# Preparing the next head's value and gate weights a head ahead, in a two-layer hybrid decoder step

## The chip, the cores and the metric

The kernel runs on one core of one Trainium2 chip. The metric is the device time of one execution in microseconds (us). The kernel before was run three times: median 2831.7 us, 2829.96 to 2833.98.

## What is computed

One step of a two-layer decoder over a prompt of 2048 positions and a sample group of 8 sequences with 4 positions each, at model width 1024, all in float32. Layer 0 is gated linear attention with 4 heads (key width 128, value width 512); layer 1 is sliding-window attention, which is not touched here. Of layer 0, cut to what matters:

```python
u = rmsnorm(h, norm_g)
proj = u @ w_in                                   # q, k, v, gate, g_low
log_a = log_sigmoid(g_low @ w_gate2 + b_gate) / 16
# for each head, chunk by chunk:
out       = (qc * exp(b)) @ state + scores @ vc
new_state = exp(b_last) * state + (kc * exp(b_last - b)).T @ vc
# then
o = rmsnorm(o, out_norm_g)
h = h + (o * silu(gate)) @ w_out
```

So each head needs its own 1024 x 512 slice of `w_in` for the values (v) and another for the gate (g), besides slices for q and k.

## The kernel before, in words

**Numbers.** Every float32 operand of a matrix product is split into two float16 parts, a high and a low one, and a product is three TensorE (PE) passes: high by high, high by low, low by high. A weight has to be *converted* so before its use: a float32 piece of 128 x 512 is loaded into one of three raw buffers (tag `wraw`), ScalarE (ACT) writes the high part, scaled by the norm's gain, and VectorE (DVE) writes the low part (`split`, lines 191 and 192, called from `Unit.convert`). A `Unit` is two such pieces, its two halves, and becomes a tile of 512 KB in one of 12 weight slots (tag `W`). The v weights of a head are four units, its gate weights four, its q and k weights together two.

**Two ways to a weight slot.** `Unit.load` converts straight into the slot. `Unit.prepare` converts each half into one of two staging buffers (tag `pst`) and writes it to a DRAM tile (`pre`) by a DMA issued from GpSimd (POOL, line 242). A unit that has been prepared answers `steps()` with a single fetch: one DMA of 512 KB from `pre` to a slot, issued from SyncE (SP). `Unit.load` and the fetch both wait until PE is done with the slot's earlier tile.

**Order of work.** Layer 0 goes through 16 blocks, four blocks of 512 positions for each of four heads (`blocks`). A block has four chunks of 128 positions. For a chunk, PE makes the v and gate projections (24 matmuls each, `vg_steps`), then the state product, the output and the state update, the norm, and the spill of the gated output (`chunk_steps`). In between, the next block's q and k projections and its seven decay levels (`level_steps`) are done. In the first three blocks of a head the two projections of a chunk run together; in a head's last block all v projections come first, then all gate projections, with the next head's v weights converted after the former and its gate weights after the latter. `weave(main, fill)` deals the closures of one list among those of another, and `mix` merges two lists in the same way. After a head's last block the 8 sample sequences of that head are done (`SampleA.steps`), woven into the first block of the next head; their state halves (`seq`) are split into the same two `pst` buffers.

**The list of conversions for later.** `prep` is a list of closures for work that layer 1 needs: eight rope tables, 72 halves of layer 1's input weights, and 64 steps that form combinations of its output weights, 144 in all. `some(n)` takes the next n. In the blocks of heads 0 to 3 the kernel takes `some(PR[j])` in each of three chunks of block j, with `PR = (1, 4, 2, 0)`: 3, 12 and 6 steps in the first three blocks of heads 1 and 2, 3 and 12 in head 3 (whose third block loads the output projection's weights instead), and 6 in the third block of head 0; 63 in all. The remaining 81 are dealt over the output projection of layer 0, seven a chunk from its fifth chunk on.

**What sets the order on the chip.** The program is built under a planner (`TileContext(nc, schedule_with_timeline_sim=True)`) that orders the instructions of each engine by priority against a simulated timeline; the closures' order gives the priorities, and `behind(steps, n)` lowers those of its steps by n. Only layer 1 pins PE's order. A tile takes the next buffer of its tag, and waits for those who use the earlier tile in that buffer. Each engine, and SP's queue of DMAs, runs its own instructions strictly in order.

Of the kernel before, what the change touches and what calls it, by code (L numbers as in the profile page):

```python
# [23 lines left out]
NBL = 4  # L24
KT = D // P
AH, DK, DV = 4, 128, 512
# [27 lines left out]
NV = 5  # L54
KL = 5
QL = 9
PR = (1, 4, 2, 0)


class Ctx:  # L60
# [14 lines left out]
def _body(tc, nc, cp, sb, ps, dr, i, o):  # L75
# [6 lines left out]
    def T(tag, shape, dt, bufs=None):  # L82
        return sb.tile(shape, dt, tag=tag, name=nm(tag), **({} if bufs is None else {"bufs": bufs}))
# [42 lines left out]
    def gain(t, src, load):  # L126
        load(t, src.rearrange("(k p) -> p k", p=P))
        dve.tensor_scalar(t, t, SW, None, ALU.mult)
# [16 lines left out]
    def weave(main, fill):  # L145

        main, fill = list(main), list(fill)
        done = 0
        for n, f in enumerate(main):
            f()  # L150
            upto = len(fill) * (n + 1) // len(main)
            for g in fill[done:upto]:
                g()
            done = upto
        for g in fill[done:]:
            g()

    def run(steps):
        for f in steps:
            f()  # L160

    def mix(a, b):

        out = []
        weave([lambda f=f: out.append(f) for f in a], [lambda f=f: out.append(f) for f in b])
        return out
# [214 lines left out]
    def u_steps(j):  # L381
        def chunk(c):
            if j > 0:
                t = T("W", [P, D], F32, NW)
                xh = [t[:, :512], t[:, 512:]]
            else:
                xh = [T("v", [P, 512], F32, 4) if c > 1 else T(tag, [P, 512], F32, 2) for tag in ("st", "sth")]
            for half in range(2):
                nc.sync.dma_start(xh[half], i["x_prompt"][0, j * 512 + c * P : j * 512 + (c + 1) * P, half * 512 : half * 512 + 512])
            norm_T(xh, P, lambda hl: uT[j][:, :, hl, c * P : (c + 1) * P], j == 0)  # L390

        return behind([lambda c=c: chunk(c) for c in range(4)], 20 if j > 0 else 0)
# [18 lines left out]
    def head_weights(h):  # L411
        w = HeadW()
        w.qk = [
            Unit([(0, P, w_in[u * 512 : u * 512 + 512, h * P : (h + 1) * P]), (P, P, w_in[u * 512 : u * 512 + 512, 512 + h * P : 512 + (h + 1) * P])], 256, gs_a, range(u * 4, u * 4 + 4))
            for u in range(2)
        ]
        w.q = lambda kt, hl: w.qk[kt // 4](kt % 4, hl, slice(0, P))
        w.k = lambda kt, hl: w.qk[kt // 4](kt % 4, hl, slice(P, 2 * P))
        w.v = Cols(w_in, 1024 + h * DV, 512, gs_a, KT)
        w.g = Cols(w_in, 3072 + h * DV, 512, gs_a, KT)  # L420
        return w
# [446 lines left out]
    def some(n=2):  # L868
        out = prep[:n]
        del prep[:n]  # L870
        return out
# [17 lines left out]
    hw = {0: head_weights(0)}  # L889
    cur = Blk(0, 0, hw[0])  # L890
# [14 lines left out]
    f = T("pst", [P, 7, 64], F32, 2)  # L905
# [16 lines left out]
    prev_tail = []  # L922
    samp = None
    sparts = []

    for n, (h, j) in enumerate(blocks):
        nxt = None
        if n + 1 < len(blocks):
            h2, j2 = blocks[n + 1]
            nxt = Blk(h2, j2, hw[h2])  # L930
        side = []
        if n == 0:
            side = u_steps(2)
        elif n == 1:
            side = u_steps(3) + [us_step]
        lv = nxt.level_steps() if nxt else []
        last = j == NBL - 1
        late = j == 0 and h > 0
        if n > 0:
            weave(cur.vg_steps(0, (0,) if late else (0, 1)), prev_tail)  # L940
        if last:
            samp = SampleA(h, cur.w)
            for f in samp.proj_steps():
                f()
        if nxt:
            for f in nxt.qk_steps():
                f()
        if late:
            weave(cur.vg_steps(0, (1,)), [])
        if last:  # L950
            ch = [cur.chunk_steps(c) for c in range(3)]
            weave([f for c in range(1, 4) for f in cur.vg_steps(c, (0,))], ch[0] + lv[:3] + ch[1][:3] + lv[3:5] + ch[2][:3])
            run(hw[h + 1].v.steps() if h + 1 < AH else wo.steps()[4:])
            for c in range(1, 4):
                weave(cur.vg_steps(c, (1,)), (ch[c - 1][3:] if c > 1 else []) + lv[3 + c * 2 : 5 + c * 2])
            for f in ch[2][3:]:
                f()
            run(hw[h + 1].g.steps() if h + 1 < AH else wo1.steps()[8:])
        else:
            for c in range(3):  # L960
                if n == len(blocks) - 2:
                    if c == 0:
                        wo_aside()
                    more = (wo1.steps()[:8] + wo.steps()[:4])[c * 4 : c * 4 + 4]
                else:
                    more = side[c * 2 : c * 2 + 2] if n < 2 else some(PR[j])
                weave(cur.vg_steps(c + 1, (0, 1) if n else (1,)), mix(cur.chunk_steps(c) + lv[(0,3,6)[c]:(3,6,8)[c]], sparts[(0,3,7)[c]:(3,7,99)[c]]) + more)
                if j == NBL - 2 and h + 1 < AH and c == 0:
                    hw[h + 1] = head_weights(h + 1)
                    for u in hw[h + 1].qk:  # L970
                        for f in u.steps():
                            f()
            sparts = []
        if n == 0:
            gain(gs_o, i["a_out_norm"][0], later)
            gain(gs_kv, i["kv_norm"], later)
            gain(gs_b, i["b_norm"][0], later)

            def bf_const(name, shape):
                f = T("pst", shape, F32, 2)  # L980
                later(f, i["c_" + name])
                t = C(name, shape, BF16)
                dve.tensor_copy(t, f)
                return t

            madd = bf_const("madd", [P, 2, P])
            nsink = C("nsink", [P, NKV * GRP], F32)
            later(nsink, i["b_sinks"][0].partition_broadcast(P))
            dve.tensor_scalar(nsink, nsink, -1.0, None, ALU.mult)
            gq = C("gq", [P, 2, HD], F32)  # L990
            for x_, g in enumerate((i["b_q_norm"][0], i["k_norm"])):
                later(gq[:, x_, :], g.partition_broadcast(P))

            lvs = C("lvs", [96, 2, 16], U8)
            f_ = T("pst", [96, 2, 16], F32, 2)
            later(f_, i["c_lvs"])
            dve.tensor_copy(lvs, f_)
            id3 = C("id3", [96, SMP], F32)
            later(id3, i["c_id3"])
            bm = C("bm", [96, NS], F32)  # L1000
            later(bm, i["c_bm"])
            onef = T("spp", [P, P], F32, 1)
            pool.memset(onef, 1.0)
            smask = bf_const("smask", [P, 2, 160])
            rts = C("rts", [SMP, 4, HD], F32)
            for y_ in range(2):
                for z_ in range(2):
                    x_ = 2 * y_ + z_
                    later(rts[:, x_, :], i["c_rope_s"][z_])
                    if z_ == 0:  # L1010
                        dve.tensor_tensor(rts[:, x_, :], rts[:, x_, :], gq[:SMP, y_, :], ALU.mult)
                    else:
                        H2 = HD // 2
                        dve.tensor_tensor(rts[:, x_, :H2], rts[:, x_, :H2], gq[:SMP, y_, H2:], ALU.mult)
                        dve.tensor_tensor(rts[:, x_, H2:], rts[:, x_, H2:], gq[:SMP, y_, :H2], ALU.mult)
            sel = T("sq1", [GRP, P], F32, 1)
            later(sel, i["c_sel"])
            skT = C("skT", [GRP, NKV], F32)
            later(skT, i["b_sinks"][0].rearrange("(g r) -> r g", r=GRP))
            psk = PT("tr", [P, NKV], bufs=2)  # L1020
            nc.tensor.matmul(psk, sel, skT, start=True, stop=True)
            sinkr = C("sinkr", [P, NKV], F32)
            dve.tensor_scalar(sinkr, psk, 8.0, None, ALU.mult)
        prev_tail = cur.chunk_steps(3) + (nxt.decay_steps() if nxt else [])
        if j == NBL - 1:
            sparts = samp.steps()
            prev_tail += sparts[:4]
            del sparts[:4]
            if nxt is None:
                prev_tail += sparts  # L1030
        cur = nxt
# [636 lines left out]
    for t in range(-3, NKV * NCH):  # L1668
        fill = []
        n = t + 3  # L1670
        if n < NKV * NCH:
            g, c = divmod(n, NCH)
# [55 lines left out]
    for p_ in range(NCH // 2):  # L1728
        more = []
        if p_ + 1 < NCH // 2:  # L1730
            nxt = pairs[p_ + 1]
            ld, sm = [lambda x=x, nxt=nxt: nxt.load(x) for x in (2, 3, 0, 1)], nxt.sums()
            more = ld[:2] + sm[:2] + ld[2:3] + sm[2:6]
# [3 lines left out]
        if p_ in (3, 4):  # L1737
            n = p_ - 3
# [87 lines left out]
```

## Time and profile before

| | |
|---|---|
| median of three runs | 2831.7 us |
| the profiled execution | 2836.73 us |
| its span, first to last instruction | 2834.9 us |
| mean granted TensorE clock | 0.986 |
| PE busy | 2716.0 us (96% of the span) |
| DVE, ACT, POOL busy | 1699.3, 1392.5, 1145.7 us |
| the 16 blocks of layer 0 end at | 1143.8 us |
| q and k, v and gate conversions of layer 0 (`wraw` from `a_w_in`) | 96 loads |
| write-outs of prepared weights (`pre` from `pst`) | 72, 256 KB each |
| fetches of prepared weights (`W` from `pre`) | 36, 512 KB each |

How it is read: a row of a table by stage has the stage's limits and length in microseconds from the span's start, then the busy time of each engine with the number of its instructions in brackets, then PE's granted clock, the busy share of the 16 DMA engines, and GB/s. When the table is asked for one tile, it counts the instructions that write or read that tile alone; an engine without any is left out, and a DMA issued by POOL counts as POOL's. A row of the waits has the engine and line that waited, what released it, then microseconds in total, times, and the longest. A row of the timeline has start, duration, engine, line, operation, out<-in, shapes and, in square brackets, how long the engine had been idle and who released it. L191 is line 191 of the kernel, and as `split` is a helper, its lines stand for every split; the tiles tell them apart.

### The profile page before, as it was taken

Reading aid. Unit: us, or ns where it says so; the run is one execution under the profiler, and the core shown is the slowest. Engines: PE = TensorE matmul, PEld = TensorE weight load, DVE = VectorE, ACT = ScalarE, POOL = GpSimd, SP = SyncE. Lnnn points to the kernel's source line nnn. Section 1 sums busy time; section 2 is a strip of 40 time slices with the busy share of each in tenths; the row PEclk is TensorE's granted clock in tenths of the full one; section 3 lists DMA queues with packets and bytes.
Section 4 is the critical chain, followed back from the end, with each engine's and each line's share of the span. In section 5 each row is a group of like instructions: output and inputs, shape, how many; then the busy total and the mean of one; then the engine's idle time right before and its main releaser. Section 6 shows DMA issues by size and latency. Waiting matters only on the chain.

```text
span 2834.9 us, 51733 instructions
## 1 busy us (share of the span) xinstructions
PE 2716.0 (96%) x19258; PEld 1388.1 (49%) x19258; DVE 1699.3 (60%) x3470; ACT 1392.5 (49%) x3245; POOL 1145.7 (40%) x1600
## 2 busy tenths in 40 slices
PE   6899998999899999999899999999999999989999
PEld 4444544544454445444344555555555555544444
DVE  5665666566657655335422665677777777777653
ACT  6554655455546553433322555566666666651110
POOL 2352244224323421125503686566567567530000
PEclk9999999999999999999999999999999999999999
DMA  8351334134313533799987678978888899996431
GB/s 210 87 128 35 101 105 148 34 86 138 116 38 86 167 90 81 184 214 260 258 183 190 129 146 152 226 133 157 187 149 151 155 189 185 177 220 201 154 99 57
DMA packets 801029, 411.69 MB, mean 145 GB/s; under 512 B 644352, under 2 KB 717896, under 8 KB 800744
## 3 DMA queue, kind: packets, MB, share of 16 engines
q1 hardware_dynamic: 787816, 372.66, 57.5%
q0 software_dynamic: 10880, 35.66, 3.7%
q8 instruction: 150, 2.46, 0.4%
q14 instruction: 103, 0.84, 0.1%
q10 hardware_dynamic: 2080, 0.07, 0.0%
HBM read 161.97 MB, written 107.54 MB: 95 GB/s over the span
## 4 chain that ended last, share of the span: by engine, by line
PE 60%; DMA 9%; ACT 9%; DVE 8%; issue 6%; POOL 5%; SPq 1%; ACTq 0%; POOLq 0%; DVEq 0%
PE pj L101 35%; PE o L101 11%; PE tr L101 9%; PE kv L101 3%; ACT o L1261 2%; DVE v L192 2%; DMA pre<-pst 1%; PE lev L101 1%; ACT v L191 1%; DMA wraw<-in_a_w_in_dram 1%; DVE o L1256 1%; POOL ogT L189 1%; DMA pst<-v 1%; DMA uT<-ogT 1%; DVE lev L1256 1%
## 5 line engine op out<-in xcount | busy, mean ns | idle before, releaser
L101 PE MATMUL pj<-W,uT 128*128 128x512 f16 x5088 | 1198.8, 381 | 6.2 <-ACT sg L481 3.6
L101 PEld LDWEIGHTS <-uT 128*128 128x128 f16 x6976 | 650.5, 98 | 711.3 <-issue 36.7
L101 PE MATMUL tr<-W,uT 128*128 128x512 f16 x1536 | 365.6, 379 | 0.0
L180 POOL TENSOR_SCALAR rs_m<-ss 128x1 f32<-128x1 f32 (+3 forms) x186 | 40.0, 215 | 537.0 <-DVE ss L1158 186.2
L101 PEld LDWEIGHTS <-X 128*128 128x128 f16 x2744 | 185.1, 98 | 141.5 <-issue 15.8
L1261 ACT ACTIVATE o<-o,mx 128x256 f32<-128x256 f32 (+1 forms) x384 | 168.7, 439 | 165.9 <-DVE mx L1256 162.0
L101 PE MATMUL pj<-uT,W 128*128 128x512 f16 (+1 forms) x912 | 190.2, 358 | 26.1 <-DMA uT<-ogT 22.6
L1256 DVE CUSTOM_DVE_ANT_0 o<-o,madd,nsink 128x256 f32<-128x256 f32 (+1 forms) x384 | 183.8, 479 | 38.6 <-PE o L101 34.2
L192 DVE SCALAR_TENSOR_TENSOR v<-o,v 128x512 f16<-128x512 f32 (+1 forms) x192 | 129.0, 672 | 104.4 <-ACT v L191 102.2
L181 POOL TENSOR_TENSOR rs_r<-rs_m,mhalf 128x1 f32<-128x1 f32 (+3 forms) x182 | 185.0, 1016 | 13.4
L514 POOL TENSOR_TENSOR KQ<-KQ,bt 128x256 f32<-128x256 f32 x112 | 97.7, 873 | 229.1 <-DVE X L189 229.1
L101 PEld LDWEIGHTS <-W 128*128 128x128 f16 x2448 | 129.6, 99 | 114.2 <-issue 23.2
L101 PEld LDWEIGHTS <-v 128*128 128x128 f16 x976 | 95.3, 98 | 116.4 <-issue 4.4
L189 POOL TENSOR_TENSOR ogT<-og,ogT 128x512 f16<-128x512 f32 x68 | 82.2, 1208 | 123.8 <-ACT ogT L188 123.8
L101 PEld LDWEIGHTS <-sg 128*128 128x128 f16 x800 | 78.4, 99 | 106.3 <-DMA sg<-ogd 11.7
L188 ACT ACTIVATE X<-KQ 128x512 f16<-128x512 f32 x128 | 84.6, 661 | 74.2 <-PE lev L101 46.8
L101 PE MATMUL o<-gl,X 128*128 128x256 f16 (+1 forms) x768 | 113.9, 271 | 3.1 <-DMA X<-qe 1.7
L189 DVE TENSOR_TENSOR X<-KQ,X 128x512 f16<-128x512 f32 x128 | 98.5, 770 | 28.4 <-ACT X L188 27.4
L191 ACT ACTIVATE v<-o 128x512 f16<-128x512 f32 (+1 forms) x192 | 111.1, 579 | 3.6
L242 POOL DMA_DIRECT2D pre<-pst x72 | 50.4, 702 | 142.2 <-DVE pst L192 111.7
L1261 ACT ACTIVATE lev<-lev,mx 128x256 f32<-128x256 f32 (+1 forms) x128 | 56.5, 441 | 103.6 <-DVE mx L1256 101.5
L101 PE MATMUL pj<-W,v 128*128 128x512 f16 x448 | 104.4, 379 | 0.4 <-DMA v<-ogd 0.4
(437 smaller groups left out, 4848.0 us busy)
## 6 DMA issues: line engine op xcount, KB each, us to landing
pre<-pst POOLq DMA_DIRECT2D x72, 256.0 KB, 3.4
W<-pre SPq DMA_DIRECT2D x36, 512.0 KB
ogd<-ogT SPq DMA_DIRECT2D x68, 256.0 KB
wraw<-in_a_w_in_dram SPq DMA_DIRECT2D x64, 256.0 KB
wraw<-in_b_w_in_dram SPq DMA_DIRECT2D x64, 256.0 KB
oge<-og SPq DMA_DIRECT2D x64, 256.0 KB
wraw<-in_a_w_out_dram SPq DMA_DIRECT2D x32, 256.0 KB
X<-in_x_prompt_dram SPq DMA_DIRECT2D x32, 256.0 KB
```

The source lines that it names most:

```text
L101: return order(nc.tensor.matmul(*a, **k))
L180: pool.tensor_scalar(m[:n, :k], ss, a, b, ALU.mult, ALU.add)
L181: pool.tensor_tensor(r[:n, :k], m[:n, :k], mhalf[:n, :k], ALU.pow)
L188: act(hi, src, AF.Copy)
L189: eng.tensor_tensor(lo, src, hi, ALU.subtract)
L191: act(hi, src, AF.Copy, scale=sc)
L192: dve.scalar_tensor_tensor(lo, src, sc, hi, ALU.mult, ALU.subtract)
L242: nc.gpsimd.dma_start(self.pre[:, :, half * 512 : half * 512 + 512], t)
L514: pool.tensor_tensor(keys, keys, d[:, :, 1:2].to_broadcast([P, NB, m]), ALU.mult)
L1256: dve.tensor_tensor_reduce(pm[:, z], pm[:, z], madd.rearrange("p a b -> p (a b)")[:, (2 - nk) * P :], -0.125, nsink[:, g * GRP + h : g * G ...
L1261: act(pm[:, z], pm[:, z], AF.Exp, scale=-1.0, bias=nm_[:, h : h + 1], accum_out=bx["sum"][:, h : h + 1])
```

## The change

`PR` goes. A list `ahead` holds the conversions that the coming blocks are to take. When head h's run begins (in its first block, for head 0 in its second), the next head's weights object is made, the 16 halves of its v and gate weights are put up for preparing, and they are mixed with steps of `prep`: 2 for head 0, 11 for heads 1 and 2. Head 3 takes 18 steps of `prep` alone. A head's last block takes 10 more (heads 0 to 2). Each chunk of the first three blocks takes three of them (`early(3)`), the last block five and then up to two a chunk. `hw[h + 1].v.steps()` and `.g.steps()` in the last block are unchanged in text, but as their units have been prepared, each is now a fetch. The q and k weights are loaded directly as before, at the same place. 120 steps are taken in the blocks, 48 of them the halves of v and gate weights, and 72 of `prep` are left for the output projection.

```diff
-PR = (1, 4, 2, 0)
...
+    ahead = []
...
         lv = nxt.level_steps() if nxt else []
+        if j == min(h, 1) ^ 1 and h + 1 < AH:
+            hw[h + 1] = head_weights(h + 1)
+            ahead = mix(hw[h + 1].v.prepare() + hw[h + 1].g.prepare(), some(11 if h else 2))
+        elif j == 0 and h > 0:
+            ahead = some(18)
+        elif j == NBL - 1 and nxt:
+            ahead = some(10)
+
+        def early(n):
+            out = ahead[:n]
+            del ahead[:n]
+            return out
+
...
-            weave([f for c in range(1, 4) for f in cur.vg_steps(c, (0,))], ch[0] + lv[:3] + ch[1][:3] + lv[3:5] + ch[2][:3])
+            weave([f for c in range(1, 4) for f in cur.vg_steps(c, (0,))], mix(ch[0] + lv[:3] + ch[1][:3] + lv[3:5] + ch[2][:3], early(5)))
             run(hw[h + 1].v.steps() if h + 1 < AH else wo.steps()[4:])
             for c in range(1, 4):
-                weave(cur.vg_steps(c, (1,)), (ch[c - 1][3:] if c > 1 else []) + lv[3 + c * 2 : 5 + c * 2])
+                weave(cur.vg_steps(c, (1,)), mix((ch[c - 1][3:] if c > 1 else []) + lv[3 + c * 2 : 5 + c * 2], early(2)))
...
-                    more = side[c * 2 : c * 2 + 2] if n < 2 else some(PR[j])
+                    more = mix(early(3), side[c * 2 : c * 2 + 2])
...
                 if j == NBL - 2 and h + 1 < AH and c == 0:
-                    hw[h + 1] = head_weights(h + 1)
                     for u in hw[h + 1].qk:
```

## The prediction

> **What bounds the kernel now.** I read the page first, then the busy time of each engine stage by stage (the edges are the gate activations that end a block, so each stage is one block of 512 positions of one head), then the same table for two tiles alone, then the waits and the timeline of one block.
>
> ```profile
> span 2834.9 us, 51733 instructions
> PE 2716.0 (96%) x19258; PEld 1388.1 (49%) x19258; DVE 1699.3 (60%) x3470; ACT 1392.5 (49%) x3245; POOL 1145.7 (40%) x1600
> ```
>
> TensorE is busy for 2716.0 of 2834.9 us, so all that any reordering of conversions can win is among 118.9 us of idle PE. The question is where these lie. In the table by stage the third number is the stage's length and the next PE's busy time:
>
> ```profile
> 143.60:206.40 62.80, 57.50 (x313) 26.50 (x312) 36.36 (x69) 34.59 (x68) 33.35 (x45) 0.97 0.57 130
> 206.40:270.30 63.90, 63.90 (x387) 30.89 (x385) 36.74 (x61) 31.23 (x56) 19.23 (x31) 1.00 0.15 41
> 270.30:337.70 67.40, 67.40 (x547) 34.65 (x546) 39.86 (x67) 37.96 (x70) 16.52 (x28) 1.00 0.22 67
> 337.70:405.80 68.10, 67.46 (x483) 33.77 (x482) 46.09 (x94) 43.32 (x77) 25.53 (x40) 1.00 0.39 113
> 405.80:480.30 74.50, 66.24 (x358) 30.57 (x356) 50.92 (x81) 46.28 (x79) 36.33 (x48) 0.98 0.55 173
> 480.30:542.60 62.30, 62.30 (x370) 29.69 (x369) 28.46 (x45) 20.42 (x38) 16.08 (x27) 1.00 0.08 22
> 542.60:608.90 66.30, 66.13 (x528) 33.73 (x526) 39.12 (x63) 37.29 (x68) 16.45 (x27) 1.00 0.23 67
> 681.50:753.30 71.80, 64.52 (x357) 30.20 (x356) 48.95 (x77) 40.58 (x72) 35.41 (x47) 1.00 0.57 180
> 815.70:882.00 66.30, 66.13 (x527) 33.71 (x526) 39.07 (x63) 37.46 (x67) 15.89 (x27) 1.00 0.26 66
> 953.00:1027.00 74.00, 66.03 (x359) 30.73 (x358) 49.25 (x77) 48.35 (x77) 33.81 (x44) 0.98 0.51 160
> 1143.80:1440.00 296.20, 279.88 (x1555) 129.56 (x1554) 129.45 (x190) 99.95 (x190) 104.56 (x140) 0.97 0.92 227
> ```
>
> Heads 1, 2 and 3 lose 8.26, 7.28 and 7.97 us in their second block (405.8, 681.5 and 953.0), together 23.5 us. Their last blocks, in which the next head's v and gate weights are converted today, lose 0.17 us each (head 0's at 270.3: nothing). So the work that the change takes out costs PE nothing where it stands. What differs in the second blocks is seen in the raw weight tile (ACT's x is the number of conversion pieces) and in the DRAM tile of prepared weights (POOL's x is the number of write-outs):
>
> ```profile
> 405.80:480.30 74.50, 17.74 (x26) 16.35 (x26) 0.00 (x0) 0.98 0.55 173
> 480.30:542.60 62.30, 0.00 (x0) 0.00 (x0) 0.00 (x0) 1.00 0.08 22
> 542.60:608.90 66.30, 10.40 (x14) 10.09 (x15) 0.00 (x0) 1.00 0.23 67
> 953.00:1027.00 74.00, 17.88 (x24) 16.90 (x24) 0.00 (x0) 0.98 0.51 160
> 405.80:480.30 74.50, 13.16 (x19) 0.98 0.55 173
> 681.50:753.30 71.80, 12.69 (x19) 1.00 0.57 180
> 953.00:1027.00 74.00, 8.43 (x13) 0.98 0.51 160
> ```
>
> **The planner does not follow the dealing.** By the source, head 1 deals 3 steps into its first block (two rope tables and one weight half), 12 into its second, 6 into its third. The rows show 19 write-outs, 1 + 12 + 6, all in the second block and none in the third: the planner runs a step as soon as an engine is free and the two staging buffers (pst) and three raw buffers come round to it. What holds a step back is who stands before it in those rings: ahead of it in the first block the sample group's state halves (they use pst too), behind it in the last block the v and gate loads, which wait for weight slots. The stage 405.8 to 480.3 is therefore a burst at the ring's pace: 74.5 / 19 = 3.9 us for each write-out.
>
> What a burst does to PE:
>
> ```profile
> ACT pst L191 <- DMA pre<-pst: 7.2, 5, 2.7
> POOL pre L242 <- DVE pst L192: 16.0, 7, 4.1
> 714.19 0.72 ACT L191 ACTIVATE pst<-wraw,gsb 128x512 f16<-128x512 f32 x1 [1.50 <-DMA pre<-pst]
> 714.82 0.61 ACT L188 ACTIVATE ogT<-og 128x512 f16<-128x512 f32 x1
> 715.52 0.72 ACT L191 ACTIVATE pst<-wraw,gsb 128x512 f16<-128x512 f32 x1
> 716.15 0.58 ACT L191 ACTIVATE v<-pj 128x512 f16<-128x512 f32 x1
> 716.78 0.38 PE L101 MATMUL kv<-v,ke 128*128 128x512 f16 x1 [1.69 <-ACT v L191]
> ```
>
> ACT stands 1.50 us at a conversion until an earlier write-out has left the staging buffer; behind it queue the og split, a second conversion and only then the v split, for which PE waits 1.69 us. POOL in the same way stands before its write-out until DVE has made the low part, with the key decay, the rsqrt and the og low part behind it. A direct conversion into a weight slot has neither wait.
>
> **The change, part by part.** *Taken out:* 16 direct half-conversions in the last block of heads 0, 1 and 2, each one ACT and one DVE pass. PE idle there is 0 + 0.17 + 0.17, so at most 0.3 us comes back, though ACT and DVE lose about 10 us of work per block.
>
> *Added:* the same 48 halves as prepared weights, at the same ACT and DVE price and a POOL write-out on top, then 24 fetches of 512 KB on SP.
>
> ```profile
> L191 ACT ACTIVATE pst<-wraw,gsb x64: 705/721/723, 433.3 to 1281.7; 128x512 f16<-128x512 f32 x64
> L192 DVE SCALAR_TENSOR_TENSOR pst<-wraw,gsb,pst x64: 733/751/1653, 434.0 to 1282.4; 128x512 f16<-128x512 f32 x64
> L242 POOL DMA_DIRECT2D pre<-pst x19: 673/682/757, 406.0 to 471.6; - x19
> DMA to landing us min/median/max: 2.6/3.2/4.5
> ```
>
> One turn of a staging buffer is 0.72 + 0.75 + 0.68 + 3.2 = 5.35 us, so two buffers yield at best one conversion per 2.7 us; 3.9 was seen. The Trainium skill, "DMA: Bandwidth & Descriptors", section on the anatomy of one DMA, gives about 2.0 us plus bytes over 436 GB/s, an estimate of 2.6 us for 256 KB. The trace's minimum agrees and its median is 0.6 us longer; by the page a turn would be 4.75 us and the burst a little milder, and the sum would lie nearer its lower end.
>
> *Moved:* dealt steps before are 3 + 12 + 6 in heads 1 and 2, 3 + 12 in head 3, 6 (all rope tables) in head 0: 63. After, 9 a block and 10 in the last: 18 + 10 in head 0 (8 rope tables, 20 weight halves), 37 in heads 1 and 2, 18 in head 3: 120. So the staging ring carries 20 more weight halves in head 0, 16 more in each of heads 1 and 2 and 3 more in head 3: 55. In heads 1 and 2, six of these stand among the sample's eight state halves in the first block. From its end on, 31 remain; nothing now stands in the rings behind the second block's steps, the v and gate loads being gone, so they run on at 3.9 us each, 121 us, through second and third blocks into the last. The second block keeps its density; the third gets one like it, with ACT 20.42 and DVE 28.46 us busy of 62.30 to take it.
>
> *Price.* Below: nothing, as with the 15 pieces in a last block. Above: all idle of the second blocks to their 51 write-outs, 23.5 / 51 = 0.46 us. I take 23.5 us over all 76 pieces converted there (26 + 26 + 24; the query and key weights wait for raw loads in the same queue), 0.31 us, nearer the upper end since new ones are of the bad kind: 55 x 0.31 = 17.0 us. A gain below nothing is the first rival.
>
> *Fetches:* v's wait for slots that PE frees in the last block, and SP's other transfers queue behind.
>
> ```profile
> SPq L217 <- DVE W L192: 146.9, 56, 18.2
> W<-pre SPq DMA_DIRECT2D x36, 512.0 KB
> ```
>
> SP stands there today too, up to 18.2 us at a raw load, and the bytes are the same (16 x 256 KB against 8 x 512). The cover is the gate's projection, 3 chunks of 24 matmuls; if it were gone, four fetches at the second block's 173 GB/s are 12 us a head. I cost them at nothing.
>
> *After the heads:* 72 steps are left for the output projection instead of 81. Its 296.20 us hold 16.3 us of idle PE, 0.20 for each of 81 steps; nine fewer give 1.8 us back.
>
> **Sum:** -0.3 + 17.0 + 0 - 1.8 = +14.9 us. The profiled execution took 2836.7 us, its span and 1.8 us around it, and is 5.0 above the median of 2831.7; so 2851.6 for a profiled run, and 2846.6 for the median.
>
> **The rivals.** *Even dealing works (faster).* If the planner leaves the steps about where they are dealt, no block sees more than 10, and the second blocks' 23.5 us go. The first block of head 1, with 4 pieces, loses 0.64 us; 13 dealt blocks at that price are 8.3. So -23.5 + 8.3 - 0.3 - 1.8 = -17.3, 2814. For it: the third block has room and loses nothing today. The Trainium skill, "Perfetto Trace Analysis", Optimization Strategy, says that where the most-contended engine changes over time, interleaving the regimes may help; that would be this. Against: the 19 write-outs in one block, and that head 0's six rope tables, dealt into its third block, stand in its second:
>
> ```profile
> L885 POOL DMA_DIRECT2D rtd<-pst x6: 901/940/1119, 158.4 to 183.9; - x6
> ```
>
> *Bursts, but free (the same).* The extra 55 fall where ACT and DVE are light and PE waits for none: -0.3 - 1.8, so 2830. For it: 15 pieces at no loss in a last block; against: those never wait for a write-out.
>
> *The sample is caught in the ring (much slower).* Six more conversions between state halves delay these by 6 x 3.9 = 23 us a head; PE runs in order, and where the planner has put a state's products ahead of a late buffer everything stands. It decides once the planner's write-out is shorter than the real one by more than its slack. One wait of 2.7 us, ACT's longest above, for each of eight state halves in three heads is 65 us; with half of it hidden, 32 on top of the forecast: 2879. Against: eight such halves pass today beside three conversions in a first block that loses 0.64.
>
> **How the numbers follow.** I give the forecast 0.47, even dealing 0.30, free bursts 0.18, the caught sample 0.05. Faster or slower means by more than 0.2%, 5.7 us, about what a measurement of this kernel can tell from no change. Faster 0.30, same 0.18, slower 0.52. The forecast's own range is 2830 (price nothing) to 2855 (55 x 0.46 = 25.3, less 2.1); as both signs have weight, the range goes from 2812, just below even dealing, to 2862, and leaves out the caught sample and the outer part of the others.
>
> **What would show it.** Right: in the prepared tile's table, heads 1 and 2 have some 15 to 19 write-outs in the second block and over ten in the third, and the third block's PE idle rises from 0 to 3 us or more, with ACT waiting for the write-out in both. The last blocks show no raw-weight pieces of v and gate, eight fetches each, and still about 0.2 us idle; the next head's v products start without a DMA wait. Write-outs rise from 72 to 120. Wrong: about 9 write-outs in each of the blocks, or a third block full of conversions without idle PE, or PE waiting for the fetches.

## The result, and the profile after

The changed kernel takes 2859.2 us (median of six runs, 2853.3 to 2864.3) against 2833.0 beside it: 1.0095 times the kernel before, 95% interval 1.0080 to 1.0109, or 26 us slower. The forecast was slower by 14.9 us, 2846.6; the range holds the time, the direction holds, the mechanism holds in the main, and the size is little more than half.

The head of the page of the profiled execution (2859.3 us) answers to the two lines at the start of the prediction:

```profile
span 2857.5 us, 51951 instructions
PE 2729.7 (96%) x19258; PEld 1393.2 (49%) x19258; DVE 1708.5 (60%) x3470; ACT 1388.7 (49%) x3242; POOL 1190.6 (42%) x1648
```

The matrix work is the same (19258 matmuls), POOL has 48 write-outs more. The 15 blocks from head 0's second to head 3's last took 1143.8 - 129.6 = 1014.2 us and now take 1171.5 - 130.5 = 1041.0: 26.8 more. What follows the blocks, 1691.1 us before, takes 1686.0. By head: 15.4 us more in head 0, 4.0 in head 1, 10.6 in head 2, 3.2 less in head 3. The table by stage, with the blocks' own edges: head 0's second, third and last block, head 1's second to last, head 2's second and third:

```profile
130.50:211.70 81.20, 70.10 (x384) 32.29 (x382) 49.73 (x92) 46.69 (x89) 33.45 (x51) 0.96 0.66 165
211.70:283.50 71.80, 65.10 (x378) 30.78 (x377) 47.24 (x71) 38.17 (x69) 44.53 (x59) 0.96 0.55 154
283.50:354.00 70.50, 70.50 (x566) 36.19 (x565) 34.59 (x58) 30.19 (x58) 16.72 (x29) 0.99 0.27 85
422.60:498.00 75.40, 69.17 (x372) 31.66 (x371) 53.03 (x84) 49.69 (x85) 39.17 (x50) 0.93 0.57 179
498.00:561.00 63.00, 62.21 (x368) 29.47 (x367) 37.12 (x57) 31.76 (x54) 25.66 (x40) 1.00 0.36 112
561.00:629.20 68.20, 68.20 (x549) 34.99 (x547) 31.24 (x52) 23.79 (x51) 15.97 (x27) 1.00 0.27 85
700.80:777.90 77.10, 66.35 (x356) 30.26 (x353) 52.84 (x82) 47.84 (x83) 35.66 (x48) 0.96 0.54 171
777.90:844.80 66.90, 64.16 (x370) 29.81 (x368) 38.81 (x60) 33.05 (x56) 28.09 (x43) 0.97 0.34 111
```

The third blocks, which lost nothing, now lose 6.70 (head 0), 0.79 and 2.74 us of PE. The second blocks of heads 1 and 2 lose 6.23 and 10.75 where they lost 8.26 and 7.28. The last blocks (283.5 and 561.0) are without a gap; before, they lost 0 and 0.17. The prepared weights' tile in these stages and in head 1's first block (354.0), POOL's x being the write-outs:

```profile
130.50:211.70 81.20, 7.80 (x11) 0.96 0.66 165
211.70:283.50 71.80, 6.26 (x9) 0.96 0.55 154
354.00:422.60 68.60, 4.25 (x6) 1.00 0.42 126
422.60:498.00 75.40, 14.65 (x21) 0.93 0.57 179
498.00:561.00 63.00, 6.87 (x10) 1.00 0.36 112
561.00:629.20 68.20, 0.00 (x0) 1.00 0.27 85
700.80:777.90 77.10, 13.90 (x20) 0.96 0.54 171
777.90:844.80 66.90, 7.68 (x12) 0.97 0.34 111
```

Dealt were 9, 9, 9 and 10 in head 1; run were 6, 21, 10 and none. And one stall of PE, from the timeline of head 2's second block, ACT's rows and then PE's:

```profile
752.67 0.91 ACT L190 ACTIVATE W<-wraw,gsa 128x256 f16<-128x256 f32 x2 [2.92 <-DMA wraw<-in_a_w_in_dram]
753.48 0.57 ACT L190 ACTIVATE v<-pj 128x512 f16<-128x512 f32 x1
754.11 0.38 PE L100 MATMUL kv<-v,ke 128*128 128x512 f16 x1 [1.98 <-ACT v L190]
```

Here it is a raw load that ACT stands at, for 2.92 us, with the v split behind. Over the blocks as a whole, though, ACT's waits at raw loads of `a_w_in` did not grow: 20.2 us before, 11.7 at weight slots and 8.0 at staging buffers now. Its waits for a staging buffer to be written out did; from 130 to 1120 us, the kernel before and then the changed one:

```profile
ACT pst L191 <- DMA pre<-pst: 23.7, 16, 2.9
ACT pst L190 <- DMA pre<-pst: 52.7, 33, 3.9
```

### The profile page after: what moved, and what is told of

The parts are those of the page before. It is cut to its first block, busy times and chain, and to the rows that moved or that the text cites. A ratio compares the mean times of both kernels' runs of the same rounds, so it can differ in the third digit from the quotient of the medians.

```text
span 2857.5 us, 51951 instructions
## 1 busy us (share of the span) xinstructions
PE 2729.7 (96%) x19258; PEld 1393.2 (49%) x19258; DVE 1708.5 (60%) x3470; ACT 1388.7 (49%) x3242; POOL 1190.6 (42%) x1648
## 4 chain that ended last, share of the span: by engine, by line
PE 55%; ACT 11%; DMA 10%; DVE 9%; issue 8%; POOL 7%; SPq 1%; POOLq 0%; ACTq 0%; DVEq 0%
PE pj L100 31%; PE o L100 10%; PE tr L100 9%; DMA pre<-pst 3%; PE kv L100 3%; ACT o L1273 2%; DVE v L191 2%; DMA wraw<-in_a_w_in_dram 2%; ACT v L190 2%; DVE pst L191 1%; PE lev L100 1%; DMA pst<-v 1%; DVE o L1268 1%; POOL ogT L188 1%; ACT pst L190 1%
## 5 line engine op out<-in xcount | busy, mean ns | idle before, releaser
L100 PE MATMUL pj<-W,uT 128*128 128x512 f16 x5088 | 1211.7, 384 | 8.6 <-ACT sg L480 4.1
L100 PE MATMUL pj<-uT,W 128*128 128x512 f16 (+1 forms) x912 | 189.5, 357 | 27.7 <-DMA uT<-ogT 24.8
L241 POOL DMA_DIRECT2D pre<-pst x120 | 84.1, 705 | 201.9 <-DVE pst L191 182.8
```

What stands on the lines that cost most here:

```text
L100: return order(nc.tensor.matmul(*a, **k))
L241: nc.gpsimd.dma_start(self.pre[:, :, half * 512 : half * 512 + 512], t)
```

## The experiments

Differences are told as ratios to the kernel before on the same chip, with their 95% intervals; microseconds given with a ratio are that share of 2832. Four questions were put: which part costs, what in a staged half costs, whether the planner's running ahead matters, and what is the best version.

| run | what it is | median us | ratio to before |
|---|---|---|---|
| e1 | preparing only | 2857.6 | 1.0087 (1.0056 to 1.0119) |
| e2 | even dealing only | 2842.2 | 1.0040 (1.0023 to 1.0057) |
| e3 | changed, 3 staging buffers | 2857.9 | 1.0086 (1.0059 to 1.0114) |
| e4 | before, 3 staging buffers | 2823.9 | 0.9977 (0.9961 to 0.9993) |
| e5 | before, 48 more passes | 2837.5 | 1.0026 (1.0013 to 1.0038) |
| e6 | e1, only head 1's weights prepared | 2838.9 | 1.0032 (1.0018 to 1.0045) |
| e7 | changed, held | 2825.6 | 0.9980 (0.9968 to 0.9992) |
| e8 | before, dealt late, held | 2836.1 | 1.0023 (1.0010 to 1.0037) |
| e9 | before, held | 2814.1 | 0.9934 (0.9921 to 0.9947) |
| e10 | e2, held | 2828.9 | 0.9987 (0.9976 to 0.9999) |
| e11 | e7, 3 staging buffers | 2831.3 | 0.9992 (0.9982 to 1.0002) |
| e12 | e1, held | 2841.0 | 1.0033 (1.0020 to 1.0047) |

**Which part.** e1 keeps the old dealing and prepares the next head's weights; its edit against the kernel before:

```diff
+        if j == min(h, 1) ^ 1 and h + 1 < AH:
+            hw[h + 1] = head_weights(h + 1)
+            ahead = hw[h + 1].v.prepare() + hw[h + 1].g.prepare()
...
-                    more = side[c * 2 : c * 2 + 2] if n < 2 else some(PR[j])
+                    more = mix(early(2 if h else 3), side[c * 2 : c * 2 + 2] if n < 2 else some(PR[j]))
```

> Only the v and gate weights are prepared a head ahead and fetched; the list for layer 1 is dealt as before (1, 4, 2, 0), so 48 more halves pass the staging ring in the blocks and 81 steps are left for the output projection. Staging theory (each half that passes the two staging buffers costs PE about 0.5 us, as 27.6 us over 55 halves in the blocks of the changed kernel, wherever it is dealt): 2833 + 24 = 2857. Dealing theory (the planner's new order through the even dealing costs, not the halves): 2833, at most 2838. Fetch theory (the fetches come late or hold up SP): 2855 as well, but then with PE idle at the heads' starts and none in the third blocks.

Measured 1.0087, about 25 us: as much as the whole slowdown, with no even dealing at all. 25 us over 48 halves are 0.51 us each; by the interval, 0.33 to 0.70.

e2 is the other half, against the changed kernel:

```diff
-            ahead = mix(hw[h + 1].v.prepare() + hw[h + 1].g.prepare(), some(11 if h else 2))
+            ahead = some(11 if h else 2)
...
-                    more = mix(early(3), side[c * 2 : c * 2 + 2])
+                    more = mix(early((2, 1, 1)[c] if h in (1, 2) else 3), side[c * 2 : c * 2 + 2])
```

> Only the dealing: v and gate weights are converted straight into their slots in the last block as before, and the list for layer 1 is dealt over all blocks in the changed kernel's amounts (2 and 10 for head 0, 11 and 10 for heads 1 and 2, 18 for head 3), 72 steps in the blocks, 7 halves more than before and 2 rope tables. Staging theory: 7 x 0.5 less what the output projection gives back (2 to 5 us): 2831 to 2836. Dealing theory: 2855 to 2860.

Measured 1.0040, 11 us, between the two theories: dealing costs too. The parts make 36 us and both together 27, which the intervals do not separate. In its stage table the first blocks of heads 1 to 3 lose 4.9, 7.3 and 6.7 us of PE, where the kernel before lost 0.6, 2.8 and 2.8.

**Fetch or staging.** e6 prepares only head 1's weights and lets heads 2 and 3 fetch them again, so that these two compute with head 1's weights, and 32 raw loads, conversions and write-outs are left out. From its edit:

```diff
+            if h == 0:
+                ahead = hw[1].v.prepare() + hw[1].g.prepare()
+            else:
+                hw[h + 1].v, hw[h + 1].g = hw[1].v, hw[1].g
```

> The prepare-only kernel, but only head 1's v and gate weights are prepared; heads 2 and 3 fetch those again (they compute with head 1's weights). 32 halves fewer pass the staging ring, and all 24 fetches stay. Staging theory: 2857.6 - 32 x 0.5 = 2842, with the third blocks of heads 1 and 2 back at no loss. Fetch theory: 2855 to 2860.

Measured 1.0032, 0.0055 below e1, about 16 us: 0.49 us for each of the 32 halves left out, though every fetch is still there. In the stage table, head 1's third block is at 62.40 of 62.40 us again, and its write-outs are 19 and 0 as before the change:

```profile
491.50:553.90 62.40, 62.40 (x370) 29.79 (x369) 29.89 (x48) 26.56 (x44) 16.45 (x27) 1.00 0.08 22
```

The same rows for the prepared weights' tile alone, x being the write-outs:

```profile
419.00:491.50 72.50, 12.80 (x19) 0.95 0.57 178
491.50:553.90 62.40, 0.00 (x0) 1.00 0.08 22
```

**Passes or write-out.** e5 adds to the kernel before the same 48 conversions into staging buffers, without write-out or fetch:

```diff
+        def passes(self):
+            def one(half):
+                t = T("pst", [P, 2, 512], F16, 2)
+                self.convert(half, lambda hl: t[:, hl])
+
+            return behind([lambda half=half: one(half) for half in range(2)], 200)
```

> The kernel before, with the 48 v and gate halves converted once more into the staging buffers where the prepare-only kernel converts them, but neither written out nor fetched (the copies are not used); the direct conversions in the last blocks stay. If the ACT and DVE passes are what displaces urgent work: 2830.5 + 24 = 2855, as with preparing. If the write-out (ACT waiting for a staging buffer that POOL has still to send) is the cost: 2830 to 2838.

Measured 1.0026, 7 us: 0.15 us a half (0.08 to 0.22) for raw load, ACT and DVE, on top of the direct conversions that stayed. By this difference the larger part of 0.51 comes with the write-out. That a staging buffer which is written out stays taken for a POOL issue and a landing longer is a likely reason, and not shown.

**A deeper ring.** e3 and e4 give the staging tag three buffers:

```diff
     def T(tag, shape, dt, bufs=None):
+        bufs = 3 if tag == "pst" else bufs
...
-                jk = T("jk2", [P, HD], BF16, 1)
+                jk = T("skn2", [P, HD], BF16, 1)
```

> The changed kernel with three staging buffers for two (a 128-byte scratch tile of layer 1 shares another's place to make room). Staging theory: ACT's waits for the write-out fall to a third or less, and with them about half of what the 55 halves cost, 2859 - 13 = 2846. If it is the ACT and DVE passes themselves that displace urgent work, not the ring: 2857 to 2861. If a faster ring only makes the burst denser: the same or slower, with more write-outs in the second blocks.

> The kernel before with three staging buffers. Staging theory: the second blocks of heads 1 to 3 get back about half of their 23.5 us, 2833 - 12 = 2821. If the passes themselves are the cost: 2831 to 2835.

e4 gains 0.23%, half of what was expected: with 18, 18 and 12 write-outs, the second blocks of heads 1 to 3 lose 15.7 us of PE together where they lost 23.5. e3 gains nothing that shows beside the changed kernel (1.0086 against 1.0095). e3's second and third blocks of head 1, write-outs and stage table:

```profile
420.40:499.50 79.10, 20.50 (x29) 0.96 0.74 235
499.50:558.10 58.60, 0.68 (x1) 1.00 0.11 34
```

The stage table of the same two blocks:

```profile
420.40:499.50 79.10, 71.05 (x382) 32.50 (x381) 57.23 (x90) 53.52 (x90) 44.29 (x58) 0.96 0.74 235
499.50:558.10 58.60, 58.60 (x342) 27.82 (x341) 30.00 (x48) 25.72 (x45) 18.72 (x30) 1.00 0.11 34
```

Its time alone would fit the second branch of the expectation, the passes, as well, but e5 puts little on these. The counts fit the third: the longer ring was used to run further ahead, 29 write-outs in the second block for 21, with 8.05 us of idle PE there for 6.23.

**The running ahead.** e7 is the changed kernel with one kind of edge more: each staged conversion may not stand on ACT before the norm of the chunk that it is dealt to (`held` is true while `Unit.prepare` converts).

```diff
             act(hi, src, AF.Copy, scale=sc)
...
+            x = act(hi, src, AF.Copy, scale=sc)
+            if held[0] and mark[0] is not None:
+                tc.add_manual_dep(x.ins, mark[0].name, mybir.DependencyInfo(mybir.DependencyClass.NoSync, mybir.DependencyReason.DATA), reason="dealt")
...
-                act(og, po, AF.Square, accum_out=ss[:, 0:1])
+                mark[0] = act(og, po, AF.Square, accum_out=ss[:, 0:1]).ins
```

> The changed kernel, with each staged conversion held on ACT behind the norm of the chunk that it is dealt to, so that the planner can't run it ahead: about 9 write-outs a block in fact. If bursts are the cost (even dealing would work if it were obeyed): 2835 or less. If the number of staged halves in the first three blocks is the cost, wherever they stand: 2853 to 2862.

Measured 2825.6, 0.9980: the same 120 steps, 0.0115 or about 33 us less than the changed kernel. Head 1's second and third block in its stage table:

```profile
414.10:481.50 67.40, 64.91 (x371) 31.01 (x370) 43.03 (x67) 40.21 (x68) 32.58 (x42) 0.97 0.39 121
481.50:549.20 67.70, 64.84 (x372) 30.30 (x371) 38.80 (x61) 34.24 (x61) 21.25 (x34) 0.97 0.34 106
```

The same rows for the prepared weights' tile alone, x being the write-outs:

```profile
414.10:481.50 67.40, 8.42 (x12) 0.97 0.39 121
481.50:549.20 67.70, 6.28 (x9) 0.97 0.34 106
549.20:618.00 68.80, 6.96 (x10) 1.00 0.49 164
```

The last row is the last block. 12, 9 and 10 for 21, 10 and none: the second block is 8 us shorter, but the third is 4.7 longer, and head 1 as a whole gains only 2.7 us. By head the blocks are 7.4, 2.7, 14.4 and 4.1 us shorter than in the changed kernel. The count theory falls, and with it the price per half as a constant. ACT's waits for the write-out, in the same stretch from 130 to 1120 us, are nearly as long as in the changed kernel (52.7 us):

```profile
ACT pst L192 <- DMA pre<-pst: 48.1, 30, 3.1
```

So the length of these waits alone does not set what PE loses. What stands behind them on ACT may, but that was not measured.

The hold was then put on the other three kernels, which completes the square.

> The kernel before, its own dealing (1, 4, 2, 0), with each staged conversion held on ACT behind the norm of its chunk as in the pinned changed kernel. If the planner's running ahead into the second block is what costs (burst theory): the second blocks fall from about 11 to 6 us of loss each, the third blocks rise to 2 or 3, 2831 - 9 = 2822, below the pinned changed kernel's 2826, since 48 fewer halves are staged. If only an even deal helps and the hold by itself does nothing: 2829 to 2834.

> The deal-only kernel (v and gate converted straight in the last blocks) with the same hold. Burst theory: 2842 - 20 = 2822, near the pinned kernel before. If preparing a head ahead is worth something once the deal is obeyed (the last blocks' free ACT and DVE): above the pinned changed kernel, 2828 or more. If a staged half still costs 0.1 us when it is dealt evenly, the 48 missing ones make it 5 us faster than the pinned changed kernel's 2825.6: 2820.

> The prepare-only kernel with the hold; it completes the square of preparing or not and dealing evenly or not, both held (2814 with neither, 2829 with dealing alone, 2825.6 with both). If a staged half still costs when it is held to its place: 48 halves at 0.5 us, 2814 + 24 = 2838. If the planner's running ahead was the whole of their cost: 2814 to 2817. Between them, at the passes' own price of 0.12 us a half that the passes-only kernel showed: 2820.

| ratio to before | neither | dealing | preparing | both |
|---|---|---|---|---|
| planner free | 1 | 1.0040 | 1.0087 | 1.0095 |
| held | 0.9934 | 0.9987 | 1.0033 | 0.9980 |

In the held row the parts clearly do not add up: dealing costs 0.0053, preparing 0.0099, both together 0.0046.

e9, the kernel before with the hold, is the fastest of all: 2814.1 us, 19 below the kernel before and 45 below the changed one. Its second and third blocks of head 1, write-outs and stage table:

```profile
407.40:476.20 68.80, 9.09 (x13) 1.00 0.41 127
476.20:536.40 60.20, 4.24 (x6) 1.00 0.31 93
```

The stage table of the same two blocks:

```profile
407.40:476.20 68.80, 68.42 (x392) 32.66 (x391) 43.22 (x66) 39.36 (x66) 31.73 (x41) 1.00 0.41 127
476.20:536.40 60.20, 58.11 (x338) 27.36 (x337) 36.86 (x59) 31.97 (x57) 20.20 (x32) 1.00 0.31 93
```

With 13 write-outs the second block loses 0.38 us of PE, with 19 it had lost 8.26; the third, with 6, loses 2.09 where it had lost nothing. ACT's wait for the write-out fell in the second block from 7.2 us in five waits to 2.1 in two, and PE's wait for ACT's v split from 2.1 us to 0.3:

```profile
ACT pst L193 <- DMA pre<-pst: 2.1, 2, 1.2
```

e12 missed all of its expected values except the highest (2841 for 2838): held, but with 19 and 12 write-outs in those two blocks of head 1, it takes 0.0099 or about 28 us more than e9, so preparing costs as much as without the hold. The old dealing with the prepared halves added puts about that many there, 18 and 12:

```profile
419.60:492.60 73.00, 13.24 (x19) 0.98 0.55 163
492.60:558.90 66.30, 8.36 (x12) 0.97 0.42 135
```

The stage table of the same two blocks:

```profile
419.60:492.60 73.00, 67.61 (x392) 31.98 (x390) 50.30 (x74) 45.67 (x77) 36.19 (x47) 0.98 0.55 163
492.60:558.90 66.30, 62.82 (x355) 29.14 (x351) 41.44 (x66) 35.82 (x64) 24.31 (x38) 0.97 0.42 135
```

So, in heads 1 to 3 of the held runs, a second block takes 12 or 13 staged halves for 0.4 to 2.8 us of idle PE (e7, e9), and 19 cost 5.4 and 5.9 (e12). Where the next head's q and k pieces come too, 12 cost 3.5 to 6.3 (third blocks of e8 and e12).

e10 gave 2828.9, not 2822, so dealing costs 15 us with the hold too. Of its expected branches the one that fits is 2828 or more, though e10 and e7 lie within each other's intervals. Its loss is not where the dealt steps are: the last blocks of heads 1 and 2 hold 25 conversions, 15 of them direct, and head 0's 19, and lose 1.2 us at most, but the next heads' first blocks, with the sample, lose 7.1, 7.2 and 6.7 us of PE where e9's lose 0.5, 1.4 and 2.5. In e7, whose last blocks have the ten dealt steps but no direct conversion, they lose 1.8, 2.2 and 3.0: that is what preparing buys once the dealing is even. The same showed in e8, which takes the whole list in the third and last blocks; from its edit against the changed kernel:

```diff
-        if j == min(h, 1) ^ 1 and h + 1 < AH:
+        if j == NBL - 2 and h + 1 < AH:
             hw[h + 1] = head_weights(h + 1)
-            ahead = some(11 if h else 2)
...
+            ahead = some(21)
```

> The kernel before (direct v and gate conversions), with the list for layer 1 taken only in the third and last blocks of heads 0 to 2, 12 and 9 steps, and held there in the same way; none in head 3, so that 81 steps become 63 in the blocks and the output projection keeps its 81. Place theory (a staged half costs little where ACT and DVE have room and much beside the sample and the q and k conversions of the second block): the second blocks' loss of some 30 us shrinks by two thirds, 2812. Count theory: 2828 to 2835.

Measured 1.0023. Head 1's first three blocks of e8, in which the first and the second hold no write-out and the third 12:

```profile
346.90:416.90 70.00, 65.26 (x449) 31.94 (x448) 45.55 (x96) 42.91 (x79) 21.23 (x34) 0.95 0.27 91
416.90:481.60 64.70, 64.70 (x375) 31.12 (x374) 30.64 (x50) 27.08 (x46) 23.46 (x28) 1.00 0.09 29
481.60:553.10 71.50, 65.83 (x362) 30.44 (x361) 42.95 (x65) 41.69 (x70) 23.44 (x38) 0.95 0.39 122
```

The second block loses nothing at all. It has neither staged halves nor q and k pieces now (those stand in the third, with 20 conversions), so its old 8.26 us were theirs together. But the loss went to the two neighbours, 4.74 and 5.67 us: the place theory's 2812 did not come out, and the time lies just above the count theory's 2828 to 2835.

> The pinned changed kernel with three staging buffers. If the waits for the write-out that are left (6.5 us of ACT in head 1's second block) still hold up PE: 2825.6 - 5 = 2820. If a conversion's wait no longer matters where it stands now: 2824 to 2828.

2831.3, 0.9992: no gain from the third buffer with the hold, and no loss that the intervals separate from e7's 0.9980. The first branch falls, and the second, 2824 to 2828, is missed by 3 us.

## Why the prediction was right, and where its size failed

*Taken out: nothing gained.* Right. The last blocks of heads 0 to 2 lost 0 to 0.17 us and lose none now; taking 15 direct pieces from each bought nothing there.

*The planner does not follow the dealing.* Right: 6, 21, 10 and none ran for 9, 9, 9 and 10 dealt in head 1. The signs came out in part: 21 and 20 write-outs in the second blocks where 15 to 19 were named, 10 and 12 in the third where it was over ten, and the third blocks' idle PE rose to 0.79 and 2.74 us, not to 3 or more, though ACT waits 7.7 and 9.9 us for write-outs there. What the running ahead costs is seen where both kernels are held: the change then costs 0.46% (e7 against e9) instead of 0.95%, about half. e7's 0.2% below the kernel before is the hold's gain and not the change's.

*Price of a staged half.* This is the step that was mis-sized. The count of 55 is itself a slip worth 0.6 us: two of head 1's 21 dealt steps before were rope tables, so its ring carries 18 more halves, not 16, and all four heads 57. 0.31 us was the second blocks' idle PE over all 76 pieces; the 15 blocks' 26.8 us over 57 halves are 0.47, and e1 and e6 measured 0.51 and 0.49. Counted in the 15 blocks alone, e1's profile has 34.4 us more than before and e6's 24.8 less than e1's, 0.72 and 0.78 a half, so the price is known to no better than 0.5 to 0.8. Two things were wrong in it. The upper bound of 0.46 was built on idle PE, and part of a stall doesn't show as idle: of the 26.8 us, 16 are idle PE, and the rest is busy time, of which the half-rate stretches below are a part. And the price was laid on as a constant, though it depends on what else is in the block. Head 0 shows it: 20 halves were to cost 6.2 us and its blocks grew by 15.4 (the second loses 11.10 us of PE for 8.31 before), beside the loading of the input's last quarter in the second and the rope tables in the third. Head 1's, forecast as 16 for 5.0, came with 4.0 us more, head 2's 16 with 10.6, and head 3's 3 with 3.2 less. More than half of the loss thus came in head 0, for which the prediction gave no reason beyond the count.

*The write-out, not the passes.* Right in kind: e5 puts 0.15 of the 0.51 us on the passes. That ACT's wait at the staging buffer is the main wait of it, as the prediction had it, is not shown: e4 speaks for a part, e3 lengthened the ring and the loss stayed, with more run ahead, and e7 won its 33 us with the waits nearly as long. POOL's wait before each write-out is no better shown. In head 1's second block of e5, ACT's and POOL's waits are 11.2 and 26.4 us against 7.2 and 16.0 before, and PE's idle is 7.84 against 8.26. A write-out by another queue, which would tell them apart, was not tried.

*Fetches at nothing.* Right. e6 keeps them and is some 16 us faster than e1. PE waited for no weight slot where a head begins; this is all that it waited for in the first 31 us of head 2 in the changed kernel:

```profile
PE kv L100 <- ACT v L190: 1.2, 1, 1.2
PE lev L100 <- DVE S L525: 0.9, 1, 0.9
PE pj L100 <- DVE v L191: 0.3, 1, 0.3
```

*After the heads: 1.8 us back.* The rest took 5.1 us less, but e1, whose output projection has all 81 steps, also spent less there than the kernel before (1679.9 us from head 3's end to the end, against 1691.1). Stretches of the program that no edit touched differ by such amounts from one profile to the next, so the nine steps' worth is not settled.

*The rivals.* Even dealing had 0.30, and its condition was false. Where the hold makes it true (e7) the second blocks of heads 1 to 3 do lose only 7.4 us for 23.5, but the time is 2825.6 rather than 2814; the steps still stand beside the sample and the q and k pieces, which may be why. The Trainium skill's advice to interleave regimes, cited there from "Perfetto Trace Analysis", Optimization Strategy, agrees with e7 against e12, the same 48 prepared halves with the list dealt evenly or as before (0.9980 against 1.0033), but not with e10 against e9 (0.9987 against 0.9934). Free bursts fell to the result, and to e1 and e6. The caught sample did not come: the first blocks of heads 1 to 3 lose 1.82, 3.64 and 3.43 us of PE, against 0.64, 2.84 and 2.77.

What stays open: which wait carries the write-out's price to PE, why 25 conversions in a last block slow the sample's block after it, and how much of the hold's gain is the spread and how much that a conversion now stands behind a chunk's norm on ACT rather than ahead of the next v split.

## What to carry to other kernels

Work moved out of a block whose bottleneck engine has no gap gains nothing in that block and can cost where it goes; read the gaps stage by stage before moving it, and count what the new route adds (here a write-out per half). Where a planner orders the engines, where a step is written is not where it runs: check the counts per stage in the trace, and if they differ from the dealing, an ordering edge on the engine that matters can be worth more than the move (19 us here, by itself). A deeper buffer ring in front of such a planner may only buy a denser burst (e3), though in the kernel before it gained 0.23% (e4).

## What the runs showed of the hardware

Short stalls can cost PE more than their length. In head 1's second block of the changed kernel, where the granted clock is 0.93, PE's timeline at three waits and after them is, with some rows left out:

```profile
488.45 0.51 PE L100 MATMUL lev<-X 128*128 128x64 f16 x12 [1.70 <-DVE S L525]
489.76 0.38 PE L100 MATMUL kv<-v,ke 128*128 128x512 f16 x1 [0.79 <-ACT v L190]
489.97 0.49 PE L100 MATMUL pj<-W,uT 128*128 128x512 f16 x1
491.76 0.59 PE L100 MATMUL kv<-v,ke 128*128 128x512 f16 x1 [1.30 <-DVE v L191]
493.00 2.77 PE L100 MATMUL pj<-W,uT 128*128 128x512 f16 x6
495.56 0.63 PE L100 MATMUL o<-v,Sh 128*128 128x512 f16 x1
497.31 0.38 PE L100 MATMUL pj<-W,uT 128*128 128x512 f16 x1
497.53 0.38 PE L100 MATMUL o<-sth,qe 128*128 128x512 f16 x1
```

Six matmuls from 493.00 to 495.56 start 0.43 us apart and take 0.63; from 497.31 on it is 0.22 and 0.38. For some 5 us PE ran at half rate, which is 2.5 us of work lost, counted as busy. The Trainium skill, "TensorE: Matmul & The Clock Gate", Part 1, has the clock fall after an idle window of about 3.4 us; here the longest single wait is 1.70 us, and the three together are 3.79 within 5 us, with matmuls between them. The same block has a second such stretch: after waits of 1.11 and 0.97 us, matmuls start 0.43 us apart from 459.7 to 462.7. So waits that lie close together can do here what one long one does.
